# Gate block steps beside other units, ScalarE copies of the activations, weight sums ahead of the splits: a transformer block on one core

## The chip, the core and the metric

One core of a Trainium2 chip runs the whole layer in one launch. The metric is the device time in microseconds (us) of one execution. Times are medians of a few runs; one more execution is run under the profiler, and the trace is of that one.

## The reference, cut to what matters

```python
D_MODEL, SEQ, D_FF = 2048, 256, 5632          # all float32, batch 1, depth 1

def _swiglu(x, wg, wu, wd):
    return (jax.nn.silu(x @ wg) * (x @ wu)) @ wd

h = h + 0.5 * _swiglu(_rmsnorm(h, ffn1_norm), ffn1_wg, ffn1_wu, ffn1_wd)
...                                            # attention and short convolution, w_in, w_out
h = h + 0.5 * _swiglu(_rmsnorm(h, ffn2_norm), ffn2_wg, ffn2_wu, ffn2_wd)
g = jax.nn.sigmoid(_rmsnorm(h, ple_norm) @ ple_w_gate)
h = h + g * (p @ ple_w_proj)
out = _rmsnorm(h, final_norm)
```

The change touches the two SwiGLU stages only. Both are the same code, `swiglu`, called for ffn1 and for ffn2.

## The kernel before

**Tiling.** There are 256 tokens, so every product has two row tiles of 128 tokens (t = 0, 1). Activations are kept transposed, 16 blocks of 128 model columns in four chunks (`aTh[c]`, `aTl[c]`). Each float32 number is held as two parts, a rounded one (hi) and what is left (lo), and each product is three matmuls (`mm3`, lines 112 to 115): hi by hi, hi by lo, lo by hi. A weight tile is 128 x 1024: SyncE fetches it (`raw`), ScalarE copies it to `whi` (line 108), and VectorE subtracts to get `wlo` (line 109, called a split below). There are six buffers each for `raw`, `whi` and `wlo`.

**Units.** The 5632 hidden columns are 11 blocks of 512. A gate, up or down unit yields one 256 x 512 result, and consists of items: an item is one weight tile and 12 matmuls (`unit_items`). A gate or up unit has 8 items, a down unit 4 for each hidden block that it sums. Gate block 0 is computed plainly. Gate blocks 1 to 10 are computed as five pairs (`Pair`) by a Strassen-like scheme with seven products in place of eight. It needs sums of weight blocks and sums of activation blocks. A pair has 12 steps: steps 0 to 7 (short steps) fetch two weight tiles, VectorE makes three sums in them (lines 344 to 346), splits both, and TensorE runs 12 matmuls; steps 8 to 11 (long steps) fetch three tiles, make two sums (line 356), three splits and 18 matmuls. After step 7 `half` takes four of the products out of PSUM; after step 11 `whole` (lines 397 to 407) makes one ScalarE copy and six VectorE sums, and queues the silu of the four results.

**Activation sums.** `factors(nm, c, p)` (lines 295 to 319) takes one 128 x 512 piece of the activations, `a`, makes four VectorE differences of 128 x 128, a ScalarE copy (hi, `sh`) and a VectorE subtract (lo, `sl`). In ffn1, `a` comes from the loaded `xT` tile by two ScalarE copies (`ffn1sa`); in ffn2 from one VectorE addition of `aTh` and `aTl` (line 306). There are eight pieces a stage. The `xT` tiles share two buffers (tag "y").

**Order of the work.** `drive` (line 172) takes a stream of items and steps, written out by hand. It prepares ahead (fetch, sums, splits) until six weight tiles are held, and then runs the oldest. Each engine executes in the order in which this emits, so that everything on VectorE, ScalarE and SyncE is a queue. Smaller work (silu, transposes) waits in `queue`; one entry is taken after the matmuls of each item (`pump`). An up unit's result is multiplied into the gate by VectorE from PSUM (line 449), transposed by TensorE and split (`pair_major`), and is then an input of the down unit. Up and down units share two PSUM banks ("mm"), so a unit can start only when the one ahead of it has been taken out.

**The schedule before.** Stage opening: gate unit 0 (8 items), up unit 0, two empty items (at the second, the queue is emptied), four down units of block 0; the 12 steps of pair 0 lie between (`merge`, lists of counts at lines 516 and 521). Then, for i = 0 to 3, a period: the two up units of pair i, with a short step of pair i+1 after every two items, and then the four down units of pair i, with a long step of pair i+1 after every four. At the end the up and down units of pair 4 alone. In ffn1, `factors` for chunks 0 to 2 are called in the preparation of gate unit 0 (`early`, line 510) and chunk 3 in that of up unit 0 (line 486). In ffn2, gate unit 0's end calls `rstd_of` (a reduction of the sums of squares on VectorE, a power on GpSimd) and the silu of gate block 0 (`silu0`).

Of the kernel before, what the change touches and what calls it, by code (L numbers as in the profile page):

```python
# [3 lines left out]

# [19 lines left out]
SEQ = 256  # L24
# [9 lines left out]
def block_kernel(ctx, tc, x, xT, pT, cols, fin, bias, mask,  # L34
# [198 lines left out]
    def next_aT(which, c, p):  # L233
# [22 lines left out]
    xraw = {}  # L256

    def load_xT(c, k0, n):
# [5 lines left out]
        for k in range(k0, k0 + n):  # L264
# [3 lines left out]
                op0=ALU.mult, op1=ALU.subtract)  # L268

# [25 lines left out]
    def factors(nm, c, p, raw=None):  # L295
# [33 lines left out]
    class Pair:  # L329
# [7 lines left out]
        def prep(self, n):  # L337
# [11 lines left out]
            rs = [fetch(w[k0, 1], f"{nm}_0"), fetch(w[k0 + 1, 1], f"{nm}_1")]  # L349
# [47 lines left out]
        def whole(self):  # L397
# [15 lines left out]
            for t in range(2):  # L413
                queue.append(partial(silu, t))

    def swiglu(nm, nxt, wg, ws, wu, wd, first):
        gate = {}
        g0 = [wk(f"{nm}sg0_{t}") for t in range(2)]

        def merge(u, pr, sched):  # L420
            s_items = pr.items()
            for cnt in sched:
                for _ in range(cnt):
                    yield next(u)
                yield next(s_items)
            assert next(u, None) is None
# [11 lines left out]
        def silu0():  # L438
            gate["rstd"] = rstd_of(nm)
# [3 lines left out]
        def up(fc, g, dst, wide=False, late=None):  # L443
            def done(pu):
                if first and fc == 0:
                    silu0()
                gs = g()
                for t in range(2):
                    stt(out=gs[t], in0=pu[t], scalar=gate["rstd"][:, t:t + 1], in1=gs[t],
                        op0=ALU.mult, op1=ALU.mult)  # L450
                dst.append(big(fc - 1 & 1, f"{nm}g{fc}"))
                for p in range(2):
                    queue.append(partial(pair_major, gs, p, f"{nm}gT{fc}", dst[-1]))
            return unit_items(wu, fc, f"{nm}u{fc}", aT, done, wide=wide, late=late)
# [25 lines left out]
        def opening():  # L480
            sets = []
            if first:
                def late(g, s):
                    load_x(g) if s == 0 else None
                    if g == 0:
                        factors(nm, 3, s, xraw[3])
                yield from up(0, lambda: g0, sets, late=late)
            else:
                yield from gate0()
                yield from up(0, lambda: g0, sets)  # L490
# [4 lines left out]
        def period(i, pr, wide=False):  # L495
            sets = []
            for j in range(2):
                yield from up(1 + 2 * i + j, lambda j=j: [pr.c[j], pr.c[2 + j]], sets, wide)
            yield from down(1 + 2 * i, 2, sets, i == 4, wide)

        def early(g, s, nm_, src):
# [394 lines left out]
```

## Time and profile before

| | |
|---|---|
| median of 3 runs | 1990.82 us (1990.23 to 1991.31) |
| profiled execution | 1991.36 us, of which the trace spans 1988.9 us |
| TensorE busy, as modelled | 1921.4 us (97% of the span) |
| VectorE busy | 1486.4 us (75%) |
| ScalarE busy | 1042.1 us (52%) |
| mean granted TensorE clock | 0.989 of full speed |
| HBM read | 433 MB, 219 GB/s over the span |

A share of the span is a mean over stages. What a change in one stage is worth is read there: from the gaps of TensorE, what ended each, and what the queue of that engine held ahead of it.

### The profile page before, as it was taken

The numbers are of one execution on the slowest core, as the hardware profiler recorded it, in microseconds if no ns is written. First come the engines' busy times: TensorE is split into PE (matmuls) and PEld (weight loads), VectorE is DVE, ScalarE is ACT, GpSimd is POOL, SyncE is SP. The second block draws the span as 40 slices with busy tenths as digits, with TensorE's granted clock in tenths as the row PEclk, the third lists the DMA queues.
The fourth block names the chain that finished last, engine by engine and source line by source line (L and its number), as shares of the span: only waits on it lengthen the run. The fifth ranks groups of instructions, "written<-read, shape, count | busy, mean of one in ns | idle before, by whom it ended". The sixth has DMA issues, their size and how long they took to land. (4 is left out here: it accounts for less than half of the span.)

```text
span 1988.9 us, 23885 instructions
## 1 busy us (share of the span) xinstructions
PE 1921.4 (97%) x8649; PEld 1577.0 (79%) x8649; DVE 1486.4 (75%) x1720; ACT 1042.1 (52%) x1305; POOL 34.8 (2%) x36
## 2 busy tenths in 40 slices
PE   7899999999999999999999979999999999999998
PEld 4677788787887888888888868787878878788887
DVE  6889789788797655656556678987977978876664
ACT  5555545555455555555445545555545545554653
POOL 0000000000000000100000000000000000000010
PEclk8899999999999999999999989999999999999999
DMA  6677768677687755544555547777676866775652
GB/s 226 240 252 245 255 216 286 227 236 249 208 276 241 237 173 189 194 167 169 180 183 177 191 148 235 257 248 263 224 252 207 285 235 227 253 248 203 204 184 98
DMA packets 127206, 437.09 MB, mean 220 GB/s; under 512 B 13808, under 2 KB 14320, under 8 KB 126832
## 3 DMA queue, kind: packets, MB, share of 16 engines
q1 hardware_dynamic: 127088, 435.57, 64.3%
q8 instruction: 68, 1.11, 0.2%
q14 instruction: 50, 0.41, 0.1%
HBM read 433.41 MB, written 2.10 MB: 219 GB/s over the span
## 5 line engine op out<-in xcount | busy, mean ns | idle before, releaser
L44 ACT ACTIVATE whi_ffn2s<-raw_ffn2s 128x1024 fp32r<-128x1024 f32 x120 | 126.4, 1060 | 124.2 <-DVE raw_ffn2s L344 81.4
L44 ACT ACTIVATE whi_ffn1s<-raw_ffn1s 128x1024 fp32r<-128x1024 f32 x120 | 126.4, 1060 | 116.4 <-DVE raw_ffn1s L344 73.3
L109 DVE TENSOR_TENSOR wlo_ffn2s<-raw_ffn2s,whi_ffn2s 128x1024 fp32r<-128x1024 f32 x120 | 145.9, 1222 | 11.6 <-ACT whi_ffn2s L44 5.5
L109 DVE TENSOR_TENSOR wlo_ffn1s<-raw_ffn1s,whi_ffn1s 128x1024 fp32r<-128x1024 f32 x120 | 145.8, 1222 | 8.1 <-ACT whi_ffn1s L44 1.4
L113 PE MATMUL ffn2u<-whi_ffn2u,aTh 128*128 128x512 f32 x352 | 138.6, 394 | 12.0 <-ACT ffn2sg L44 11.9
L114 PE MATMUL ffn1u<-wlo_ffn1u,aTh 128*128 128x512 f32 x352 | 137.4, 390 | 2.9 <-DVE wlo_ffn1u L109 2.9
L113 PE MATMUL ffn1u<-whi_ffn1u,aTh 128*128 128x512 f32 x352 | 138.2, 393 | 0.6 <-ACT whi_ffn1u L44 0.5
L109 DVE TENSOR_TENSOR wlo_ffn2d<-raw_ffn2d,whi_ffn2d 128x1024 fp32r<-128x1024 f32 x88 | 106.6, 1223 | 42.0 <-ACT whi_ffn2d L44 40.5
L109 DVE TENSOR_TENSOR wlo_ffn1d<-raw_ffn1d,whi_ffn1d 128x1024 fp32r<-128x1024 f32 x88 | 106.6, 1223 | 41.8 <-ACT whi_ffn1d L44 40.1
L115 PE MATMUL ffn2u<-whi_ffn2u,aTl 128*128 128x512 f32 x352 | 137.7, 391 | 0.0
L114 PE MATMUL ffn2u<-wlo_ffn2u,aTh 128*128 128x512 f32 x352 | 137.7, 391 | 0.0
L115 PE MATMUL ffn1u<-whi_ffn1u,aTl 128*128 128x512 f32 x352 | 137.1, 390 | 0.0
L44 ACT ACTIVATE whi_ffn2d<-raw_ffn2d 128x1024 fp32r<-128x1024 f32 x88 | 92.0, 1057 | 70.2 <-PE ffn2d L115 33.7
L44 ACT ACTIVATE whi_ffn1d<-raw_ffn1d 128x1024 fp32r<-128x1024 f32 x88 | 92.3, 1057 | 68.7 <-PE ffn1d L115 33.6
L109 DVE TENSOR_TENSOR wlo_ffn2u<-raw_ffn2u,whi_ffn2u 128x1024 fp32r<-128x1024 f32 x88 | 104.5, 1219 | 21.1 <-ACT whi_ffn2u L44 20.7
L109 DVE TENSOR_TENSOR wlo_ffn1u<-raw_ffn1u,whi_ffn1u 128x1024 fp32r<-128x1024 f32 x88 | 104.6, 1219 | 20.1 <-ACT whi_ffn1u L44 20.1
L44 ACT ACTIVATE whi_ffn2u<-raw_ffn2u 128x1024 fp32r<-128x1024 f32 x88 | 89.2, 1049 | 23.6 <-PE ffn2d L115 11.2
L44 ACT ACTIVATE whi_ffn1u<-raw_ffn1u 128x1024 fp32r<-128x1024 f32 x88 | 89.2, 1048 | 21.4 <-PE ffn1d L115 11.2
L113 PEld LDWEIGHTS ffn2u<-whi_ffn2u,aTh 128*128 128x128 f32 x352 | 66.6, 189 | 26.4 <-ACT ffn2sg L44 12.3
L114 PEld LDWEIGHTS ffn1u<-wlo_ffn1u,aTh 128*128 128x128 f32 x352 | 66.3, 188 | 17.1 <-DVE wlo_ffn1u L109 3.5
L113 PEld LDWEIGHTS ffn1u<-whi_ffn1u,aTh 128*128 128x128 f32 x352 | 66.2, 188 | 15.3 <-ACT whi_ffn1u L44 1.3
L115 PEld LDWEIGHTS ffn2u<-whi_ffn2u,aTl 128*128 128x128 f32 x352 | 66.5, 189 | 14.0
(795 smaller groups left out, 5106.8 us busy)
## 6 DMA issues: line engine op xcount, KB each, us to landing
raw_ffn1s<-in_ws SPq DMA_DIRECT2D x120, 512.0 KB, 5.6
raw_ffn2s<-in_ws SPq DMA_DIRECT2D x120, 512.0 KB, 5.5
raw_ffn1u<-in_wu SPq DMA_DIRECT2D x88, 512.0 KB, 5.2
raw_ffn1d<-in_wd SPq DMA_DIRECT2D x88, 512.0 KB, 4.8
raw_ffn2u<-in_wu SPq DMA_DIRECT2D x88, 512.0 KB, 5.2
raw_ffn2d<-in_wd SPq DMA_DIRECT2D x88, 512.0 KB, 4.8
raw_o<-in_wout SPq DMA_DIRECT2D x32, 512.0 KB, 3.9
raw_pg<-in_wpg SPq DMA_DIRECT2D x24, 512.0 KB, 4.6
```

Source lines behind the costliest of these rows:

```text
L44: nc.scalar.activation(out=out, in_=in_, func=func, **kw)
L109: tt(out=lo[:, sl], in0=raw[:, sl], in1=f(hi[:, sl]), op=ALU.subtract)
L113: nc.tensor.matmul(ps, lhsT=xh, rhs=wh, start=first, stop=False)
L114: nc.tensor.matmul(ps, lhsT=xh, rhs=wl, start=False, stop=False)
L115: nc.tensor.matmul(ps, lhsT=xl, rhs=wh, start=False, stop=last)
```

## The change

The arithmetic of the products stays the same, with the same weights, matmuls and transposes. What is done otherwise:

1. The steps of a pair move. The short steps of pair i+1 now lie between the items of the down units of pair i (one after every two), and its long steps between the items of its own up units (before the 1st and 5th item of the first up unit, and the 1st and 3rd of the second). The places of the 60 steps of a stage are given as positions in one stream.
2. The first up unit of a pair (`up_a`) ends before the pair's gate. It is copied out of PSUM by ScalarE (`ua`); after the silu, `after` multiplies the two in SBUF on VectorE. The second (`up_b`) is multiplied from PSUM as before.
3. The two halves of a transposed hidden block are queued as one entry (`turned`) in place of two.
4. `factors` reads a ScalarE copy (`keep`, tiles `full`), made where the activations are made: in ffn1 right behind each `xT` load, in ffn2 from the PSUM tile of the transposes. All eight `factors` of ffn1 move to the preparation of up unit 0.
5. In ffn2, `rstd_of` is called before gate unit 0.
6. In the long steps the fetch of the third tile and the two sums come ahead of the splits of the other two.

```diff
@@ next_aT, line 246
+            if which == "ffn2":
+                keep(c, k, ps[:, kk * 256:(kk + 1) * 256], g)
@@ line 256
+    full = {}
+    def keep(c, k, src, g):
+        p = k // 2
+        if (c, p) not in full:
+            full[c, p] = wk(f"a{c}_{p}")
+        act(full[c, p][:, (k % 2) * SEQ:(k % 2 + 1) * SEQ], src, scale=g)
@@ load_xT, line 268
+            keep(c, k, raw[:, k, :], g)
@@ factors, line 295
-    def factors(nm, c, p, raw=None):
+    def factors(nm, c, p):
...
-        a = wk(f"{nm}sa{c}_{p}")
-        k = 2 * p
-        if raw is None:
-            tt(out=a, in0=f(aTh[c][:, k:k + 2, :].rearrange("p k s -> p (k s)")),
-               in1=f(aTl[c][:, k:k + 2, :].rearrange("p k s -> p (k s)")), op=ALU.add)
-        else:
-            for i in range(2):
-                act(a[:, i * SEQ:(i + 1) * SEQ], raw[:, k + i, :],
-                    scale=col[:, c * 4 + k + i:c * 4 + k + i + 1])
+        a = full.pop((c, p))
@@ Pair.prep, line 348
-            rs = [fetch(w[k0, 1], f"{nm}_0"), fetch(w[k0 + 1, 1], f"{nm}_1")]
             t1 = raw_tile(f"{nm}_t")
             nc.sync.dma_start(out=t1.rearrange("p (k c) -> p k c", k=2),
                               in_=w[k0:k0 + 2, 0, :, 0:512].rearrange("k p c -> p k c"))
-            us = [split(rs[d], f"{nm}_{d}") for d in range(2)]
+            rs = [fetch(w[k0, 1], f"{nm}_0"), fetch(w[k0 + 1, 1], f"{nm}_1")]
             for d in range(2):
                 sl = slice(d * 512, (d + 1) * 512)
                 tt(out=t1[:, sl], in0=t1[:, sl], in1=rs[d][:, 0:512], op=ALU.add)
+            us = [split(rs[d], f"{nm}_{d}") for d in range(2)]
@@ Pair.whole, line 413
             for t in range(2):
                 queue.append(partial(silu, t))
+            queue.append(self.after)
+            queue.append(self.turn)
@@ swiglu (merge, up, opening and period are taken out)
         def silu0():
-            gate["rstd"] = rstd_of(nm)
+            if first:
+                gate["rstd"] = rstd_of(nm)
...
+        def turned(gs, fc, dst):
+            dst.append(big(fc - 1 & 1, f"{nm}g{fc}"))
+            def turn(d=dst[-1]):
+                for p in range(2):
+                    pair_major(gs, p, f"{nm}gT{fc}", d)
+            return turn
+        def gated(pu, gs):
+            for t in range(2):
+                stt(out=gs[t], in0=pu[t], scalar=gate["rstd"][:, t:t + 1], in1=gs[t],
+                    op0=ALU.mult, op1=ALU.mult)
+        def up0(sets, late=None):
+            def done(pu):
+                if first:
+                    silu0()
+                gated(pu, g0)
+                queue.append(turned(g0, 0, sets))
+            return unit_items(wu, 0, f"{nm}u0", aT, done, late=late)
+        def up_a(fc, pr, sets):
+            def done(pu):
+                ua = [wk(f"{nm}ua{fc}_{t}") for t in range(2)]
+                for t in range(2):
+                    act(ua[t], pu[t], scale=gate["rstd"][:, t:t + 1])
+                pr.ua = ua
+            return unit_items(wu, fc, f"{nm}u{fc}", aT, done)
+        def up_b(fc, pr, sets):
+            def done(pu):
+                gs = [pr.c[1], pr.c[3]]
+                gated(pu, gs)
+                queue.append(turned(gs, fc, sets))
+            return unit_items(wu, fc, f"{nm}u{fc}", aT, done)
+        def pair(i):
...
+            def after():
+                for t in range(2):
+                    tt(out=pr.c[2 * t], in0=pr.ua[t], in1=pr.c[2 * t], op=ALU.mult)
+                pr.turn_a = turned([pr.c[0], pr.c[2]], 1 + 2 * i, pr.sets)
+        def opening(pr):
...
                 def late(g, s):
-                    load_x(g) if s == 0 else None
-                    if g == 0:
-                        factors(nm, 3, s, xraw[3])
+                    if s == 0:
+                        load_x(g)
+                    factors(nm, g, s)
...
+        def plain_stream(prs):
+            yield from opening(prs[0])
+            for i in range(5):
+                yield from down(1 + 2 * i, 2, prs[i].sets, i == 4, i == 4)
+                if i < 4:
+                    yield from ups(i + 1, prs[i + 1])
@@ early, line 509
-            if g > 0:
-                factors(nm, g - 1, s, xraw[g - 1])
@@ everything
             if first:
                 yield from gate0(early)
-                sched = [2, 2, 1, 1, 1, 1, 1, 1, 2, 2, 2, 2]
+                at = [6, 8, 9, 10, 12, 14, 16, 18, 20, 24, 26, 29]
+                base = 34
             else:
+                gate["rstd"] = rstd_of(nm)
...
-                sched = [4, 3, 2, 3, 2, 2, 1, 1, 2, 2, 2, 2]
+                at = [6, 8, 11, 14, 16, 17, 18, 20, 22, 24, 26, 34]
+                base = 42
...
+                places += [base + 32 * i + o for o in (0, 2, 4, 6, 8, 10, 12, 14, 16, 20, 24, 26)]
```

`opening` ends with the two up units of pair 0, and a step stands before the item of the stream that its place names. In ffn1 the stream begins behind gate unit 0, in ffn2 with it.

## Rows read from the trace of the kernel before

**Rows 1.** The page, part 1: busy us, share of the span, instructions.

```profile
PE 1921.4 (97%) x8649; PEld 1577.0 (79%) x8649; DVE 1486.4 (75%) x1720; ACT 1042.1 (52%) x1305; POOL 34.8 (2%) x36
```

**Rows 2.** TensorE's waits: waiter, releaser, total us, how many, longest.

```profile
PE ffn2u L113 <- ACT ffn2sg L44: 11.9, 1, 11.9
PE ffn1g L113 <- ACT whi_ffn1g L44: 10.3, 4, 3.5
PE ffn1s0q L113 <- ACT ffn1sg L44: 7.2, 1, 7.2
...
PE ffn1s1q L114 <- DVE wlo_ffn1s L109: 1.0, 1, 1.0
...
PE ffn1d L113 <- ACT ffn1g4h L44: 0.9, 1, 0.9
...
PE ffn1d L115 <- DVE ffn1g4l L203: 0.6, 1, 0.6
...
PE ffn1s3q L114 <- DVE wlo_ffn1s L109: 0.4, 1, 0.4
```

**Rows 3.** Stretches: length, busy us of PE, PEld, DVE, ACT, POOL; PEclk, DMA, GB/s.

```profile
6.80:46.20 39.40, 29.84 (x96) 21.61 (x96) 27.52 (x60) 23.28 (x48) 2.57 (x2) 0.83 0.64 223
...
63.30:69.40 6.10, 6.06 (x14) 4.84 (x15) 4.54 (x6) 3.76 (x5) 0.00 (x0) 0.50 0.88 342
...
409.00:538.80 129.80, 127.89 (x570) 104.95 (x569) 107.20 (x117) 67.88 (x71) 0.00 (x0) 1.00 0.72 243
```

**Rows 4.** Timeline of TensorE where two stretches end: start, us, instruction.

```profile
148.21 0.39 PE L113 MATMUL ffn1u<-whi_ffn1u,aTh 128*128 128x512 f32 x1
148.44 0.39 PE L114 MATMUL ffn1u<-wlo_ffn1u,aTh 128*128 128x512 f32 x1
...
408.98 0.39 PE L113 MATMUL ffn1u<-whi_ffn1u,aTh 128*128 128x512 f32 x1
```

**Rows 5.** Waits of SyncE's DMA queue, first 70 us.

```profile
SPq L262 <- ACT ffn1sa L44: 19.4, 2, 10.0
```

**Rows 6.** Timeline of ScalarE in up unit 0 of ffn1.

```profile
45.13 0.63 ACT L44 ACTIVATE ffn1sh<-ffn1sv 128x512 fp32r<-128x512 f32 x1 [1.21 <-DVE ffn1sv L317]
...
49.12 0.63 ACT L44 ACTIVATE ffn1sh<-ffn1sv 128x512 fp32r<-128x512 f32 x1 [1.61 <-DVE ffn1sv L317]
```

**Rows 7.** Timeline of VectorE, one short step and two up items.

```profile
327.00 0.68 DVE L344 TENSOR_TENSOR raw_ffn1s<-raw_ffn1s,raw_ffn1s 128x512 f32<-128x512 f32 x1
...
331.54 2.35 DVE L109 TENSOR_TENSOR wlo_ffn1u<-raw_ffn1u,whi_ffn1u 128x1024 fp32r<-128x1024 f32 x2
333.81 0.69 DVE L344 TENSOR_TENSOR raw_ffn1s<-raw_ffn1s,raw_ffn1s 128x512 f32<-128x512 f32 x1
```

**Rows 8.** Timeline of VectorE, the last sum of `whole`, pair 2 of ffn1.

```profile
411.23 0.69 DVE L407 TENSOR_TENSOR ffn1s2c<-ffn1s2q,ffn1s2c 128x512 f32<-128x512 f32 x1
```

**Rows 9.** Timeline of VectorE, gate block 0 of ffn1: `rstd_of`, gating, lo of its transposes.

```profile
97.76 0.21 DVE L224 TENSOR_REDUCE sm_ffn_None<-ss_ffn 128x1 f32<-128x4 f32 x2
...
101.15 0.68 DVE L344 TENSOR_TENSOR raw_ffn1s<-raw_ffn1s,raw_ffn1s 128x512 f32<-128x512 f32 x1
...
107.96 1.28 DVE L203 TENSOR_TENSOR ffn1g0l<-ffn1gT,ffn1g0h 128x512 fp32r<-128x512 f32 x2
```

**Rows 10.** Timeline of ScalarE at the start of the down units of pair 2.

```profile
484.45 1.06 ACT L44 ACTIVATE whi_ffn1s_t<-raw_ffn1s_t 128x1024 fp32r<-128x1024 f32 x1 [2.73 <-issue]
485.41 0.58 ACT L44 ACTIVATE ffn1g6h<-ffn1gT 128x512 fp32r<-128x512 f32 x1
```

**Rows 11.** Timeline of ScalarE, opening of ffn2.

```profile
1146.04 0.19 ACT L44 ACTIVATION_READ_ACCUMULATOR junk_ffn<-h 128x1 f32 x1
...
1149.26 0.47 ACT L44 ACTIVATE aTh<-trh_ffn,col 128x256 fp32r<-128x256 f32 x1 [0.55 <-DVE aTl L244]
...
1181.56 1.28 ACT L44 ACT_TABLE_LOAD   x1
1184.32 1.26 ACT L44 ACTIVATE ffn2sg<-ffn2g,rstd_ffn_None 128x512 f32<-128x512 f32 x2 [1.48 <-POOL rstd_ffn_None L230]
```

More of the change, by code (lines that the diff above doesn't have):

```diff
@@ L3 @@
 from functools import partial
+from itertools import chain
 import concourse.bass as bass
@@ L418, in swiglu @@
         g0 = [wk(f"{nm}sg0_{t}") for t in range(2)]
[L420 to L426, printed above, removed]
         def gate0(early=None, late=None):
@@ L444, in done @@
+        def gated(pu, gs):
[3 more added lines that the diff above has]
+        def up0(sets, late=None):
             def done(pu):
-                if first and fc == 0:
+                if first:
                     silu0()
-                gs = g()
-                for t in range(2):
-                    stt(out=gs[t], in0=pu[t], scalar=gate["rstd"][:, t:t + 1], in1=gs[t],
-                        op0=ALU.mult, op1=ALU.mult)
@@ L451, in done @@
[L451 to L454, printed above, removed]
+                gated(pu, g0)
[4 more added lines that the diff above has]
+                ua = [wk(f"{nm}ua{fc}_{t}") for t in range(2)]
+                for t in range(2):
+                    act(ua[t], pu[t], scale=gate["rstd"][:, t:t + 1])
+                pr.ua = ua
+            return unit_items(wu, fc, f"{nm}u{fc}", aT, done)
@@ new lines, in up_b @@
+        def up_b(fc, pr, sets):
[5 more added lines that the diff above has]
+        def pair(i):
+            pr = Pair(nm, ws, i, gate)
+            pr.sets = []
+            def after():
+                for t in range(2):
+                    tt(out=pr.c[2 * t], in0=pr.ua[t], in1=pr.c[2 * t], op=ALU.mult)
+                pr.turn_a = turned([pr.c[0], pr.c[2]], 1 + 2 * i, pr.sets)
+            pr.after = after
+            pr.turn = lambda: pr.turn_a()
+            return pr
@@ L456, in swiglu, with ups @@
+        def ups(i, pr):
+            yield from up_a(1 + 2 * i, pr, pr.sets)
+            yield from up_b(2 + 2 * i, pr, pr.sets)
         class Lazy:
@@ L478, in nothing @@
             return 0, None, lambda _: fn() if fn is not None else None
-        def opening():
+        def opening(pr):
             sets = []
@@ L483, in late @@
                 def late(g, s):
-                    load_x(g) if s == 0 else None
-                    if g == 0:
-                        factors(nm, 3, s, xraw[3])
-                yield from up(0, lambda: g0, sets, late=late)
+                    if s == 0:
+                        load_x(g)
+                    factors(nm, g, s)
+                yield from up0(sets, late)
             else:
                 yield from gate0()
-                yield from up(0, lambda: g0, sets)
+                yield from up0(sets)
             yield nothing()
@@ L493, in opening @@
             yield from down(0, 1, sets, False)
[L495 to L499, printed above, removed]
+            yield from ups(0, pr)
+        def plain_stream(prs):
[4 more added lines that the diff above has]
+                    yield from ups(i + 1, prs[i + 1])
         def early(g, s, nm_, src):
@@ L520, in everything @@
                         queue.append(partial(factors, nm, c, p))
-                sched = [4, 3, 2, 3, 2, 2, 1, 1, 2, 2, 2, 2]
-            pr = Pair(nm, ws, 0, gate)
-            yield from merge(opening(), pr, sched)
+                at = [6, 8, 11, 14, 16, 17, 18, 20, 22, 24, 26, 34]
+                base = 42
+            prs = [pair(i) for i in range(5)]
+            places = list(at)
             for i in range(4):
-                nx = Pair(nm, ws, i + 1, gate)
-                yield from merge(period(i, pr), nx, [2] * 8 + [4] * 4)
-                pr = nx
-            yield from period(4, pr, True)
+                places += [base + 32 * i + o for o in (0, 2, 4, 6, 8, 10, 12, 14, 16, 20, 24, 26)]
+            u = plain_stream(prs)
+            n = 0
+            steps = chain.from_iterable(pr.items() for pr in prs)
+            for place in places:
+                while n < place:
+                    yield next(u)
+                    n += 1
+                yield next(steps)
+            yield from u
         drive(everything())
```

1 line of the change is left out of this document (removed).

## Prediction, made before the changed kernel was run

> **What bounds the kernel now.** I read the busy times first: TensorE is busy 97% of the span, VectorE 75%, ScalarE 52% [rows 1]. Within a unit the matmuls start 0.227 us apart [rows 4], so an item or short step (12 matmuls) takes 2.72 us and a long step (18) 4.08; the change alters no matmul, so only TensorE's gaps can be won or added. They are 1988.9 - 1921.4 = 67.5 us in all. The table of TensorE's waits says where. First, single large gaps: gate unit 0 of ffn1 waits 10.3 us in four pieces for its copies, then 7.2 us for one ScalarE copy; up unit 0 of ffn2 waits 11.9 us for the silu of gate block 0 [rows 2]. Second, a small pattern: in each of the eight periods the first down unit waits 0.9 + 0.6 us for the second hidden block, and most periods begin with 0.4 to 1.2 us for a VectorE subtract [rows 2]. The table of stretches shows a whole period: 129.8 us with 127.9 of TensorE, so 1.9 to win [rows 3]. It shows, third, what a large gap costs besides itself: the granted clock was at 0.50 (the 1.2 GHz level) in the 6.1 us behind the 7.2 us gap, which is 3 us of work lost, and 0.83 on average in gate unit 0, whose longest gap is 3.5 us [rows 2, 3].
>
> So the sum has five terms. Each is how long VectorE and ScalarE, as queues, keep TensorE waiting in a stretch under the new order. My prices on VectorE: a pair of items and a short step 333.81 - 327.00 = 6.81, of which two items 2.27 (their row's 2.35 less the overlap at its end), so a short step 4.5 [rows 7]. TensorE needs 8.16 for the same.
>
> **1. Opening of ffn1.** Now the third and fourth chunk of `xT` wait 19.4 us in SyncE's queue until `ffn1sa` has read the first two [rows 5]. The copies by `keep` read them at once, so this wait goes, and six `factors` leave gate unit 0. An item of the gate unit then takes ScalarE two hi and two `keep` copies of 0.47 [rows 11] and two of half a tile, 1.06 / 2 [rows 10]: 2.9, or 2.65 with 0.05 of overlap at each, about TensorE's 2.72. At the 342 GB/s of the busiest row [rows 3] the inputs of five items, 0.79 MB each, and two bias tiles take 13 us, so I estimate the fifth item's landing at 17 and the gate unit's preparation to end at 28 (four items on); TensorE ends it at 31 in place of 46.
>
> But VectorE gets all eight `factors` in up unit 0. Such an item with its factor repeats every 49.12 - 45.13 = 4.0 us [rows 6], because subtract, differences, ScalarE copy and subtract wait for each other. From 28 on VectorE's queue is: first factor's copy at 31.4; seven more at 4.0, 28; squares and gate copies on ScalarE in between, 2; step 0, 4.5; to 66.9 with the last factor. Then steps 1 and 2, 9; `rstd_of` and gating, 101.15 - 97.76 = 3.4 [rows 9]; step 3, two down items, step 4, 4.5 + 2.3 + 4.5: 90.5. Only then comes the lo part of the transposed gate block (0.6 to its first half, 1.28 for both [rows 9]), because the preparation runs six tiles ahead and the transposes are emitted as the second empty item is run, behind step 4's preparation. The first down item needs it: TensorE, ready at 85, waits until 91, some 5.5 us, and I add 2.5 for the clock. The second down item ends at 91 + 2.3 + 2.7 + 2.5 = 98.5. Left are 26 units of 2.72, four long steps and transposes: 98.5 + 70.7 + 16.3 + 0.9 = 186.4. Now the same work is done at 148.2 [rows 4] plus 16 up items and transposes, 192.6. **Gain 6.3.** Bounds: -6 (half clock in the starved up unit as well, below) to +14 (the lo part is not late).
>
> **2. Periods, the gap that goes.** ScalarE copied the hi part of the second transposes (485.41) behind the copy of the third tile of a long step (484.45), which had waited for its sums [rows 10]. Behind the change both transposes are made after the first down item, a short step lies before they are needed, and weight sums come first. The wait at a period's start goes too: six up items now lie behind `whole`. Eight times 1.55, six times 0.35, two times 1.25 [rows 2]: **gain 17.0.**
>
> **3. Periods, the wait that is new.** `after` is taken from `queue` three items behind step 11, and VectorE has in front of it: `whole`, three up subtracts, and the next pair's step 0. `whole` ends 411.84 - 408.98 = 2.9 us behind step 11 [rows 4, 8]; three subtracts 3.4; step 0 4.5; two products of 0.6: 12.0. TensorE reaches the transposes of this block after four items, 10.9. So it stands 1.1 us, behind it everything else. The silus (ScalarE, done by 5) are not last. There is no step 0 behind pair 4, and in ffn2 pair 0 has eight items there; seven waits remain. **Loss 8.0.** No row shows this wait; the nearest ones are the 0.9 and the 1.4 + 1.1 us by which such queues are late now, so 0 to 2.5 each, 0 to 17 in all. In the down units VectorE needs 2 x 6.81 + 1.28 for two sums into `h` = 14.9 per four items and two steps, TensorE 16.3, so I cost it at nothing; it enters with six tiles in hand.
>
> **4. Opening of ffn2 to up unit 0.** `rstd_of` is now the first VectorE work of the stage, and the emission order chains everything of the stage behind it. It needs the squares of the last chunk, done at 1146.2 [rows 11], so subtracts that now are made ahead start at 1146.8, and TensorE stands 3 us there. `next_aT` of the last chunk gets `keep` copies. The second hi copy starts 0.55 us late, when VectorE's read of the same PSUM tile has ended [rows 11], so with `keep` the three reads of a column go one by one, 1.42 us in place of 1.03: 5.7 for four. VectorE's queue from 1146.8: six subtracts 6.8, four columns to 1158.3, step 0 4.5, two factors with items 8.0, two factors 5.1, step 1: its copy at 1177.7, its first subtract at 1179.2. TensorE gets there at 1173.2, waits, and ends step 1 at 1181.6. The silu is behind four copies and a table load (1.28), 1.26 long [rows 11]: done about 1184.4. Up unit 0 starts at 1184.1 in place of 1185.1, at full clock sooner: **gain 2.5**, -6 to +12 (nothing waits at 1145, and the silu finds its factor ready).
>
> The Trainium skill (PSUM — Partial Sum Buffer, "PSUM bank collisions raise a hardware error") says that no two engines may use one bank and quadrant at once, reads beside reads included. The rows agree: by it the sum is as above; if the copies could run beside VectorE, step 1 would be 1.6 us sooner and the total 1976.4.
>
> **5. Opening of ffn2, first down unit.** As in 1, the lo of gate block 0 is emitted behind the preparation of step 7. From the end of up unit 0: gating 0.8, step 6 4.5, two items 2.3, step 7 4.5, lo 0.6: 12.5; TensorE is there at 9.2. It waits 3.3, and I charge 2 for the clock, since the 3.5 us gap is the nearest. Now there are 0.9 us. **Loss 4.4**, 0 to 8.
>
> The rest I cost at nothing: `ua` (0.6 us copies) is hidden by the long step behind it, the gating of `up_b` by step 0, `h` by a short step each. DMA moves the same bytes. In the last down units the first one takes the other PSUM banks.
>
> **Sum** against the profiled execution: 1991.4 - 6.3 - 17.0 + 8.0 - 2.5 + 4.4 = **1978.0 us**. That execution lies 0.5 above the median, which is less than my rounding.
>
> **Rivals.** (a) The new waits don't come: ScalarE and VectorE reach `after` and the lo parts in time. For it: in term 3 the margin is 1 us, and TensorE has four items of cover. Against: three queues would have to be short at once. Without term 3, and with terms 1, 4 and 5 at +10, +4 and 0: 1960. (b) Openings give nothing: up unit 0 of ffn1 is starved to 68% for 35 us and its clock halves. Then an item takes 5.1 us in place of VectorE's 4.0, eight of them 9 us more: 1987. Against it: these gaps are of 1 to 2 us, half of the smallest behind which I saw it fall. The same time comes out if `xT` is not what paces gate unit 0, that is if the change doesn't do there what it says. (c) Slower: the products of `after` are later than I count, because VectorE comes late to step 11 by a preparation. Every 1 us more is 7 us in all. At 1.9 more, 3.0 each, the gain is gone; with two more items' subtracts in its way (2.3) it is 7 x 2.3, and at gaps of 3.4 us each 7 x 2 for the clock: 2008. For it speaks that VectorE runs without a pause for 60 us of a period now; against it, that these are short steps beside up items, and step 11 now has light work ahead.
>
> **How the numbers follow.** Forecast 0.53, (a) 0.16, (b) 0.19, (c) 0.12. The forecast's own range is 1969 to 1986, from its terms' bounds taken together. With 8 in 10 I reach from (a) to just above (b): 1961 to 1992. A difference under 0.2%, 4 us, can't be told from none: faster is the forecast, (a), and a little of (b), 0.71; same most of (b), 0.17; slower (c), 0.12.
>
> **What would show it.** The wait for `ffn1sa` gone from SyncE's queue, and gate unit 0 done by 31 to 33; TensorE waiting for `wlo` in up unit 0 with gaps of 1 to 2 us; one gap near 5 us at the first down item of ffn1, for `ffn1g0l`; none of 0.9 + 0.6 at the down units, and seven of about 1 us at transposes, released by VectorE's products; in ffn2 a gap of 3 us at 1145, one before step 1, one at the first down item, none of 11.9. I am wrong if the transposes wait 3 us or more, or if the clock is at half through up unit 0.

## The result, and the profile after

The changed kernel takes **1967.92 us** (median of 3, 1966.44 to 1968.21) against 1990.82: a ratio of 0.9883 (95% interval 0.9861 to 0.9906). The gain is 22.9 us; 13.4 were forecast. Its profiled execution took 1967.92 us with a span of 1965.8.

The page of the kernel after, part 1 (busy us, share of the span, instructions), answers to [rows 1]:

```profile
PE 1920.9 (98%) x8649; PEld 1583.5 (81%) x8649; DVE 1475.8 (75%) x1712; ACT 1054.9 (54%) x1341; POOL 36.2 (2%) x36
```

The same matmuls are busy for the same time; all that changed lies between them. TensorE's waits of the kernel after (waiter, releaser, total us, how many, longest), beside [rows 2]:

```profile
PE ffn2g L115 <- DVE wlo_ffn2g L110: 3.4, 1, 3.4
PE ffn1s0q L114 <- ACT whi_ffn1s L45: 3.2, 3, 2.0
PE ffn1s0q L115 <- DVE wlo_ffn1s L110: 3.1, 4, 1.0
PE ffn2d L114 <- ACT ffn2g0h L45: 2.4, 1, 2.4
PE ffn1g L114 <- ACT whi_ffn1g L45: 2.4, 1, 2.4
PE ffn1d L114 <- ACT ffn1g0h L45: 2.3, 1, 2.3
PE ffn2s0q L114 <- ACT whi_ffn2s L45: 2.3, 1, 2.3
PE ffn1u L115 <- DVE wlo_ffn1u L110: 2.2, 3, 0.8
...
PE ffn1gT L292 <- DVE ffn1s0c L483: 1.8, 2, 1.6
...
PE ffn1gT L292 <- DVE ffn1s1c L483: 0.8, 2, 0.6
```

Of the 11.9 before up unit 0 of ffn2 0.6 is left, and of the 10.3 in gate unit 0 one wait of 2.4 at its start; the 7.2 before step 0 and the sixteen waits of 0.9 and 0.6 are gone. In their place stand the waits that the prediction named: 3.4 at the start of ffn2, one before step 1 of ffn2 (`ffn2s0q`), one at each first down item, and one at the transposes of seven pairs (`ffn1s0c` 1.8, six others 0.8). The largest that it did not price is 6.3 in all at the first steps of pair 0 in ffn1 (`ffn1s0q`). A stretch of gate unit 0, the 24 us behind it with most of up unit 0, and one whole period, from one pair's first transpose to the next pair's, beside [rows 3]:

```profile
core 0: us, PE busy (x) PEld busy (x) DVE busy (x) ACT busy (x) POOL busy (x), PEclk, DMA share, GB/s
8.00:32.00 24.00, 24.00 (x95) 19.41 (x95) 19.05 (x36) 21.34 (x46) 0.00 (x0) 1.00 1.00 368
32.00:56.00 24.00, 19.71 (x75) 14.54 (x73) 17.30 (x31) 13.28 (x28) 3.16 (x2) 0.93 0.59 208
...
310.05:438.21 128.16, 127.34 (x569) 105.28 (x569) 106.41 (x117) 68.38 (x73) 0.00 (x0) 1.00 0.73 246
```

From 8 us on gate unit 0 of ffn1 now runs without a gap, with all DMA engines busy. The period is 128.16 us in place of 129.8. (A down unit has two items for each hidden block that it sums, so four in a period, and not four for each block.)

**Where the time came from.** The last matmul of the output projection ends 13.5 us sooner (1130.25 against 1143.72), and from there to the first matmul behind ffn2 (`pp`) it is 9.6 us less (726.2 against 735.8). So ffn1 gives 13.5 and ffn2 9.6, where the terms of the forecast make 10.2 and 3.2.

### The profile page after: what moved, and what is told of

It reads as the page before. It is cut to its first block, busy times and chain, and to the rows that moved or that the text cites. A ratio compares the mean times of both kernels' runs of the same rounds, so it can differ in the third digit from the quotient of the medians.

```text
span 1965.8 us, 23881 instructions
## 1 busy us (share of the span) xinstructions
PE 1920.9 (98%) x8649; PEld 1583.5 (81%) x8649; DVE 1475.8 (75%) x1712; ACT 1054.9 (54%) x1341; POOL 36.2 (2%) x36
## 4 chain that ended last, share of the span: by engine, by line
PE 88%; DVE 6%; ACT 3%; issue 2%; DMA 1%; ACTq 0%; POOL 0%; SPq 0%; POOLq 0%; DVEq 0%
PE ffn1d L116 4%; PE ffn2d L116 4%; PE ffn2d L114 4%; PE ffn1d L114 4%; PE ffn2d L115 4%; PE ffn1d L115 4%; PE ffn2u L114 4%; PE ffn2u L116 4%; PE ffn2u L115 3%; PE ffn1u L114 3%; PE ffn1u L116 3%; PE ffn1u L115 3%; PE o L116 1%; PE o L114 1%; PE o L115 1%
## 5 line engine op out<-in xcount | busy, mean ns | idle before, releaser
L110 DVE TENSOR_TENSOR wlo_ffn1d<-raw_ffn1d,whi_ffn1d 128x1024 fp32r<-128x1024 f32 x88 | 104.6, 1220 | 11.1 <-ACT whi_ffn1d L45 10.3
L114 PEld LDWEIGHTS ffn2u<-whi_ffn2u,aTh 128*128 128x128 f32 x352 | 66.1, 188 | 14.8 <-ACT ffn2sg L45 1.3
L116 PEld LDWEIGHTS ffn1u<-whi_ffn1u,aTl 128*128 128x128 f32 x352 | 66.7, 189 | 13.9
```

The costliest lines, as they stand in the source:

```text
L110: tt(out=lo[:, sl], in0=raw[:, sl], in1=f(hi[:, sl]), op=ALU.subtract)
L114: nc.tensor.matmul(ps, lhsT=xh, rhs=wh, start=first, stop=False)
L116: nc.tensor.matmul(ps, lhsT=xl, rhs=wh, start=False, stop=last)
```

## Experiments

Each time is a median of four runs with the kernel before on the same chip; ratios are to that. The runs were made on four chips, and the kernel before had medians of 1989.99 to 1991.53 us there, so a difference between two kernels from different chips is good to 1 or 2 us. All spans and stretches come from one trace each.

### Which part brings it: the sums or the schedule

My theory for the periods named both: ScalarE's copy of the third tile waits for the sums, and the moved steps take the transposes out of its way. Two kernels separate them. The kernel before with the sums first alone:

```diff
-            rs = [fetch(w[k0, 1], ...), fetch(w[k0 + 1, 1], ...)]
             t1 = raw_tile(f"{nm}_t")
             nc.sync.dma_start(out=t1..., in_=w[k0:k0 + 2, 0, :, 0:512]...)
-            us = [split(rs[d], f"{nm}_{d}") for d in range(2)]
+            rs = [fetch(w[k0, 1], ...), fetch(w[k0 + 1, 1], ...)]
             for d in range(2):
                 tt(out=t1[:, sl], in0=t1[:, sl], in1=rs[d][:, 0:512], op=ALU.add)
+            us = [split(rs[d], f"{nm}_{d}") for d in range(2)]
```

> The kernel before with one part of the change alone: in the four long steps of a pair the two weight sums stand ahead of the first two splits. Theory A (the 0.9 + 0.6 us at the first down unit of a period come from ScalarE's copy of the third tile, which waits for sums that stand behind two subtracts): these sixteen waits go, 12.4 us as listed and up to 4 more if each wait also costs a refill of some 0.27 us that the table of waits does not count; 1974 to 1980. Theory B (the waits come from where the long steps and the second transposes lie in the order, and only the moved steps take them away): within 2 us of the kernel before, 1989 to 1991, waits of 0.9 + 0.6 still there.

Measured: **1971.32 us** (0.9905, 0.989 to 0.992). And the changed kernel with these lines as they were before (the same diff backwards):

> The changed kernel with the weight sums of the long steps behind the two splits again, as before: the schedule of the change without the sums. The kernel before with the sums alone gave 1971.3, a steady period of 128.2 us instead of 129.8. Theory A (sums first is what the periods live on; the moved steps bring nothing by themselves): 1978 to 1984, periods of 129 us or more. Theory B (either of the two takes the 0.9 + 0.6 us away, since the moved steps take the transposes out of the way of the third tile's copy): 1967 to 1971, periods near 128.2.

Measured: **1977.85 us** (0.9931, 0.9915 to 0.9948). So the sums alone gain 18.7, the schedule and the rest alone 13.7, both together 22.9: they overlap, and the few lines of the sums are the larger part. VectorE's subtract of the third tile shows why; the last part is the idle time ahead of its twenty instructions in ffn1. The kernels before, with the schedule alone, with the sums alone, and after:

```profile
L109 DVE TENSOR_TENSOR wlo_ffn1s_t<-raw_ffn1s_t,whi_ffn1s_t 128x1024 fp32r<-128x1024 f32 x20 | 24.5, 1225 | 25.1 <-ACT whi_ffn1s_t L44 25.1
```

```profile
L110 DVE TENSOR_TENSOR wlo_ffn1s_t<-raw_ffn1s_t,whi_ffn1s_t 128x1024 fp32r<-128x1024 f32 x20 | 24.5, 1225 | 25.1 <-ACT whi_ffn1s_t L45 25.1
```

```profile
L109 DVE TENSOR_TENSOR wlo_ffn1s_t<-raw_ffn1s_t,whi_ffn1s_t 128x1024 fp32r<-128x1024 f32 x20 | 24.5, 1223 | 9.4 <-ACT whi_ffn1s_t L44 9.4
```

```profile
L110 DVE TENSOR_TENSOR wlo_ffn1s_t<-raw_ffn1s_t,whi_ffn1s_t 128x1024 fp32r<-128x1024 f32 x20 | 24.4, 1221 | 3.2 <-ACT whi_ffn1s_t L45 3.1
```

With the sums behind two subtracts VectorE stands still for 25.1 / 20 = 1.26 us in each long step, since subtract, sums, copy and subtract follow each other. The moved schedule leaves this bubble as it is: the first matmul of an up item then waits for a bank that VectorE empties late, 0.9 us a period (`h` as releaser), where the kernel before waited 0.9 and 0.6 for transposes. With sums first alone two small waits a period are left. TensorE's waits in the middle of ffn1, schedule alone, then sums alone:

```profile
PE ffn1u L114 <- DVE h L509: 3.8, 4, 1.2
```

```profile
PE ffn1s2q L114 <- DVE wlo_ffn1s L109: 0.4, 1, 0.4
...
PE ffn1d L115 <- DVE ffn1g2l L203: 0.2, 1, 0.2
```

Theory A held for the sums in its mechanism, and the gain was larger than its range by 2.7 us; that rest isn't assigned. Of the second run theory A held in its time (0.15 below its range) and its period (129.24), but its words that the moved steps bring nothing by themselves did not: here too the waits of 0.9 and 0.6 are gone, only others of 0.9 and 0.8 stand in their place, and the kernel gains 13.7. And one thing that neither expected: a period with sums alone is 128.20 us, with the whole change 128.16. **In steady state the moved steps, as they stand in the change, bring nothing over the sums**, and in ffn2 as a whole they and the rest don't either (725.6 against 726.2 us); what they give back in waits at down items they spend at the new transposes. What the schedule, the copies and the moved `factors` have of their own is the 4.2 us in ffn1, whose opening they shorten.

### The new wait at the transposes, and what a wait costs

Theory: the two products of `after` stand behind the next step 0's sums and subtracts. First, that step one item later:

```diff
-at = [6, 8, 9, 10, 12, 14, 16, 18, 20, 24, 26, 29]
+at = [6, 8, 9, 10, 12, 14, 16, 18, 20, 24, 26, 28]
-places += [base + 32 * i + o for o in (0, 2, 4, ...)]
+places += [base + 32 * i + o for o in (1, 2, 4, ...)]
```

> The changed kernel with the first step of the next pair one item later (and step 11 of pair 0 in ffn1 one item sooner), so that the two products stand ahead of that step's sums on VectorE. Theory A (the products are late by what VectorE has to prepare ahead of them): all seven waits at the transposes go. The table lists 6.7 us for them; if a wait costs 0.16 us ahead of it and 0.2 to 0.3 behind it on top of what is listed, the gain is 9.5. So 1958.5 against 1961.2 tells whether the listed time is the whole cost. Theory B (it is the silu or the ua copy, or the step moved is late in its turn): 1965 to 1968, the waits still there or as much at the first step of a pair.

Measured: **1961.88 us** (0.9860, 0.9845 to 0.9874), 6.0 less than the changed kernel. The seven waits are gone (theory A), but a small one of 0.26 stands at eight first down items, since the transposes end too close ahead of them. So the run doesn't decide between 1958.5 and 1961.2: with these eight taken off, listed waits alone would give 4.6 us, and 5.7 with the prices that the table below gives, too near to each other for two chips. The periods in that table decide it.

One of the eight:

```profile
PE ffn1d L114 <- DVE ffn1s1c L451: 0.3, 1, 0.3
```

So the same effect by another edit, which also brings the transposes one item forward (like the run above and all kernels built on this one, it has step 11 of pair 0 in ffn1 one item sooner, 28 in place of 29):

```diff
-            for t in range(2):
-                queue.append(partial(silu, t))
+            queue.append(lambda: (silu(0), silu(1)))
             queue.append(self.after)
```

> The changed kernel with both silus of a pair as one entry of the queue (and step 11 of pair 0 in ffn1 one item sooner): products and transposes both come one item earlier. In the run with step 0 one item later the waits at the transposes went, but 0.26 us at the first down item came in their place, for the hi half of this block. Theory A (that hi half was one item short of time): no wait at the transposes nor at the first down item, 1958 to 1960. Theory B (VectorE reaches the products too late for transposes that are one item earlier): 1962 to 1968, waits for products at the transposes.

Measured: **1960.33 us** (0.9844, 0.983 to 0.9859), 7.6 less, theory A, 0.3 above its range; between 100 and 680 us TensorE has no wait at all, and elsewhere three of 0.21 at transposes are left. Its period of 126.91 us is 1.29 below that of the sums alone: with this edit the moved steps do bring something in steady state. It is the yardstick for the others. Period from the first transpose of pair 1 to that of pair 2 in ffn1 (the two gaps of 0.60 and 0.21 at one pair's transposes count as one wait of 0.81):

| kernel | waits listed in it, us | how many | period, us | over 126.91 |
|---|---|---|---|---|
| before | 0.91 + 0.64 + 0.35 = 1.90 | 3 | 129.80 | 2.89 |
| schedule alone | 0.81 + 0.88 = 1.69 | 2 | 129.24 | 2.33 |
| sums alone | 0.22 + 0.36 = 0.58 | 2 | 128.20 | 1.29 |
| after | 0.81 | 1 | 128.16 | 1.25 |
| step 0 later | 0.26 | 1 | 127.43 | 0.52 |
| silus together | none | 0 | 126.91 | 0 |

Every period is longer than its listed waits by 0.26 to 0.44 us for each of them. The records around a wait show it, here TensorE at a transpose wait of the kernel after (start us, length, line, operation, tiles, count, idle before and releaser):

```profile
308.84 0.39 PE L115 MATMUL ffn1u<-wlo_ffn1u,aTh 128*128 128x512 f32 x1
309.06 0.39 PE L116 MATMUL ffn1u<-whi_ffn1u,aTl 128*128 128x512 f32 x1
310.05 0.30 PE L292 MATMUL ffn1gT<-ident,ffn1s1c 128*128 128x128 f32 x1 [0.60 <-DVE ffn1s1c L483]
310.56 0.98 PE L292 MATMUL ffn1gT<-ident,ffn1s1c 128*128 128x128 f32 x7 [0.21 <-DVE ffn1s1c L483]
```

Back to back, matmuls start 0.22 to 0.23 apart. Here 0.99 lie between the last one and the transpose: 0.60 are listed as idle, and 0.16 more are the end of a matmul that otherwise lies beside the next one's start. The transposes behind the wait start further apart as well. **A wait that TensorE runs into costs its listed time and about 0.27 us** (0.44 for the two gaps at one pair's transposes).

### The opening of ffn1: the factors or the release of `xT`

Term 1 said that gate unit 0 was held by `xT`'s slow release and by six `factors`. First the changed kernel with these six back in gate unit 0, `xT` still free at once:

```diff
             out = split(raw, nm_, 2)
+            if g > 0:
+                factors(nm, g - 1, s)
...
-                    factors(nm, g, s)
+                    if g == 0:
+                        factors(nm, 3, s)
```

> The changed kernel with the factors of the first three chunks of xT back in gate unit 0 of ffn1, where the kernel before had them, but still from the copies, so that xT is free at once. Theory A (the opening is bound by VectorE's sum of work, wherever the factors lie): gate unit 0 ends at 36 to 40 us instead of 32.5, up unit 0 has no waits, and the whole is 1964 to 1969. Theory B (xT's release alone paced gate unit 0 and its factors cost nothing there): it still ends by 33, the waits of up unit 0 and of step 0 go: 1957 to 1961. Theory C (factors in gate unit 0 make it the bound): 1971 or more.

Measured: **1970.25 us** (0.9894, 0.988 to 0.9909). Gate unit 0 ends at 45.6, 13 us later, and yet the whole is only 2.3 longer: theory C in the gate unit, and in the whole between the ranges of A and C. Then the other cause, as it was meant: the kernel before with sums first and the differences of the `factors` on GpSimd, `xT` released as slowly as it was:

```diff
+    pt = nc.gpsimd.tensor_tensor
-        tt(out=v[:, 0], in0=a21, in1=a22, op=ALU.subtract)
+        pt(out=v[:, 0], in0=a21, in1=a22, op=ALU.subtract)
```

(and so for the other three)

> The kernel before with the weight sums first (1971.3 us) and the differences of the factors on GpSimd; none of the moved steps, copies or reductions of the change. Theory A (VectorE's work in the factors is what paced gate unit 0 of ffn1, whatever the schedule): gate unit 0 ends at 34 to 38 us in place of 46, the 5.6 us before step 0 shrink: 1956 to 1963. Theory B (in the old schedule xT's slow release paces the gate unit, so the factors' cost is hidden): gate unit 0 still ends near 46, 1968 to 1972.

Measured: **1978.21 us** (0.9942, 0.9925 to 0.9958), slower than the sums alone by 6.9. Gate unit 0 still ends at 46.8, as theory B said, but the time is 6 us above its range: up unit 0 of ffn2 waits 15.2 us in place of 11.9, and ffn1 is 2.9 longer than with the sums alone. The last starts of gate unit 0, and what stood in the way: SyncE's queue, and VectorE's subtract of the factors (idle time ahead of it, 8 to 66 us). After; factors back; before; sums and GpSimd:

```profile
L114 PE MATMUL ffn1g<-whi_ffn1g,aTh x32: 388/390/794, 7.6 to 31.6; 128*128 128x512 f32 x32
```

```profile
L114 PE MATMUL ffn1g<-whi_ffn1g,aTh x32: 387/396/628, 7.5 to 44.1; 128*128 128x512 f32 x32
...
SPq L100 <- DVE wlo_ffn1g L110: 15.4, 4, 4.3
```

```profile
L319 DVE TENSOR_TENSOR ffn1sl<-ffn1sv,ffn1sh 128x512 fp32r<-128x512 f32 x8 | 5.8, 729 | 7.4 <-ACT ffn1sh L44 4.9 <-ACT ffn1sa L44 2.5
```

```profile
L114 PE MATMUL ffn1g<-whi_ffn1g,aTh x32: 389/397/795, 7.2 to 45.9; 128*128 128x512 f32 x32
...
PE ffn2u L114 <- ACT ffn2sg L44: 15.2, 1, 15.2
...
SPq L263 <- ACT ffn1sa L44: 20.0, 2, 10.4
...
L320 DVE TENSOR_TENSOR ffn1sl<-ffn1sv,ffn1sh 128x512 fp32r<-128x512 f32 x8 | 6.2, 780 | 20.9 <-ACT ffn1sh L44 16.6 <-ACT ffn1sa L44 4.3
```

With the factors back, the wait for `ffn1sa` of [rows 5] is gone from SyncE's queue; it waits for VectorE's subtracts instead, and TensorE ends the unit as late as before. So the six factors alone are enough for the 46 us. What they cost is their chain: copy, differences, copy (`ffn1sh`) and subtract go from engine to engine, and the hi copies of successive weight tiles start 5.17 us apart, where TensorE needs 2.72 for a tile. Freeing `xT` does give something that TensorE doesn't show: the last hi copy of the unit starts at 38.9 in place of 42.5, but the granted clock is at 0.50 from 39.8 to 46.6.

The run with GpSimd does not isolate the other cause. It takes the differences off VectorE but leaves them in the chain, and VectorE stands idle 20.9 us ahead of the factors' subtract in place of 7.4. The hi copies of successive tiles start 5.34 us apart where no transfer is waited for, against 4.5 in the kernel before. **That the factors in gate unit 0 hold it is shown; that the slow release of `xT` would hold it alone is not.** First down items show what counts further on: 90.4 us in the kernel after and 92.3 with the factors back, though gate unit 0 ends 13 us later. That agrees with VectorE's work bounding this opening wherever it lies, so less of it should show at once under the new schedule.

### Less work for VectorE, and the start of ffn2

In ffn2 the reductions of `rstd_of` stood ahead of six subtracts that could have been made earlier:

```diff
-                gate["rstd"] = rstd_of(nm)
...
-                yield from gate0()
+                def stat(g, s):
+                    if (g, s) == (2, 1):
+                        gate["rstd"] = rstd_of(nm)
+                yield from gate0(late=stat)
```

> The changed kernel with the reductions of ffn2's scale emitted behind the first six preparations of gate unit 0 instead of ahead of all. Theory A (the 3.4 us at the start of ffn2 and the half clock behind it are the price of a VectorE queue that stands behind the last squares): the wait goes, VectorE is 6 us sooner through the gate unit, 1961 to 1964. Theory B (VectorE's work up to the silu is what counts, and the time comes back in front of step 1 or of the silu): 1966 to 1968, with a longer wait there.

Measured: **1961.60 us** (0.9854, 0.9838 to 0.9871), 6.3 less: theory A. The 3.4 us are gone, and the wait before step 1 is what it was, not longer (2.3). With the silus together as well:

> The changed kernel with the silus as one entry and with the reductions of ffn2's scale behind the first six preparations. The two touch different stretches, so theory A: gains add, 6.3 of the reductions and 6 to 9.5 of the silus: 1952 to 1956. Theory B (one of them only moves a wait): 1958 to 1962.

Measured: **1955.44 us** (0.9820, 0.9805 to 0.9834), 12.5 less than the change: the two nearly add. On this kernel, the four differences on GpSimd:

> The kernel with silus together and reductions later (1955.4 us), with the four differences of every factor (128x128, 0.28 us each on VectorE) made on GpSimd, in both openings. Theory A (the openings are bound by VectorE's sum of work): 1.1 us less for each of eight factors in ffn1 and four in ffn2, waits of up unit 0 and of the first steps smaller, first down item of ffn1 4 to 8 us earlier: 1946 to 1951. Theory B (VectorE's queue stands still while it waits for the differences, so what GpSimd takes longer comes back): 1954 to 1962, VectorE idle before the factors' subtract.

Measured: **1935.88 us** (0.9725, 0.971 to 0.9739), a further 19.6, more than twice what I expected. Theory A's mechanism, mis-sized: I had taken 1.1 us for a factor. In this kernel `a` is made early, and GpSimd runs ahead of VectorE: the differences of five factors are done by 21.8 us, while gate unit 0 is still running. VectorE's groups up to 90 us, without and then with GpSimd:

```profile
L322 DVE TENSOR_TENSOR ffn1sl<-ffn1sv,ffn1sh 128x512 fp32r<-128x512 f32 x8 | 5.5, 693 | 6.4 <-ACT ffn1sh L45 6.4
...
L317 DVE TENSOR_TENSOR ffn1sv<-a 128x128 f32<-128x128 f32 x8 | 3.4, 421 | 0.0
L318 DVE TENSOR_TENSOR ffn1sv<-a 128x128 f32<-128x128 f32 x8 | 3.4, 421 | 0.0
...
L319 DVE TENSOR_TENSOR ffn1sv<-a,ffn1sv 128x128 f32<-128x128 f32 x8 | 2.3, 292 | 0.3
L320 DVE TENSOR_TENSOR ffn1sv<-a,ffn1sv 128x128 f32<-128x128 f32 x8 | 2.3, 292 | 0.3
```

```profile
L323 DVE TENSOR_TENSOR ffn1sl<-ffn1sv,ffn1sh 128x512 fp32r<-128x512 f32 x8 | 6.0, 752 | 3.0 <-ACT ffn1sh L45 3.0
```

The differences are 3.4 + 3.4 + 2.3 + 2.3 = 11.4 us, and VectorE stood 6.4 us waiting for its own chain to come back from ScalarE; now 3.0. That is 14.8 us of its queue, and the output projection ends 13.0 sooner. ffn2 gives 6.8: the wait before step 1 and the half clock behind it are gone.

### The first down item

Both openings have a wait of some 3 us at the first down item. Theory: the lo half is emitted behind a step. First the changed kernel with one step moved:

```diff
-at = [6, 8, 9, 10, 12, 14, 16, 18, 20, 24, 26, 29]
+at = [6, 8, 9, 10, 14, 16, 17, 18, 20, 24, 26, 29]
-at = [6, 8, 11, 14, 16, 17, 18, 20, 22, 24, 26, 34]
+at = [6, 8, 11, 14, 16, 17, 18, 22, 23, 24, 26, 34]
```

> The changed kernel with one gate block step in each opening moved behind two more down items (ffn1: step 4 from place 12 to 14, ffn2: step 7 from 20 to 22, the next ones closed up), so that the lo half of the first transposed gate block stands behind two subtracts of 1.15 us instead of a whole step of 4.5. Theory A (order of emission makes the first down item wait): both waits fall from 3.0 to about 0.8 us and the half clock behind them goes, 4.4 + 2 to 3.4 us: 1960 to 1962. Theory B (VectorE has a backlog there, so the step that was moved is late instead): 1965 to 1968, with new waits at that step.

Measured: **1966.85 us** (0.9882, 0.9867 to 0.9896), 1.1 less, which is within the scatter: theory B. The waits split up and move on. TensorE at the first down items of ffn1, kernel after, then this one:

```profile
PE ffn1d L114 <- ACT ffn1g0h L45: 2.3, 1, 2.3
PE ffn1d L116 <- DVE ffn1g0l L204: 0.6, 1, 0.6
```

```profile
PE ffn1d L114 <- DVE h L509: 2.4, 2, 1.6
PE ffn1d L116 <- DVE ffn1g0l L204: 1.4, 1, 1.4
```

Then ffn2's steps spread over more items (`[6, 8, 11, 13, 16, 17, 20, 22, 23, 24, 26, 34]`, on the kernel of 1955.44):

> The same kernel (1955.4 us) with the gate block steps of ffn2's opening spread: step 3 one item sooner, step 6 behind the second down item, step 7 behind the fourth. VectorE then has one step and two items in front of the lo half of the first gate block, 6.8 us, in place of 11.3. Theory A (five steps close together are more than VectorE can do beside them): the 2.7 + 0.65 us at the first down item and the half clock behind go, 1950.5 to 1952.5. Theory B (as where the step alone was moved back: the lateness moves to the next items): 1954 to 1956.

Measured: **1953.26 us** (0.9813, 0.9797 to 0.983): 2.2 less, between the theories (the intervals of the two ratios overlap; in the traces ffn2 takes 715.9 us in place of 718.5); 1.8 + 1.0 us are left of 2.7 + 0.65. At last all of these together, ffn1's steps sooner too (`[4, 6, 8, 9, 10, 13, 16, 18, 20, 24, 26, 28]`):

> The kernel with silus together, reductions later and the differences on GpSimd (1935.9 us), with the steps of both openings spread: ffn2's as in the run before (it gave 2.2 us), ffn1's from 6, 8, 9, 10, 12, 14 to 4, 6, 8, 9, 10, 13, since VectorE is now free in up unit 0. Theory A (VectorE's lateness at the first down item is the last large gap, 4.6 us with half clock behind it in ffn1): that gap falls below 2, ffn2's as in the run before: 1927 to 1931. Theory B (transfers or VectorE in up unit 0 are the next bound): waits come back in up unit 0, 1933 to 1936.

Measured: **1935.36 us** (0.9727, 0.9713 to 0.9742), no different from the 1935.88: theory B. The 4.6 us at the first down item become 0.6, and 2.9 at a step ahead of it and 2.7 at a later down item take their place. Order alone did little in these three runs, where VectorE has a backlog; what helped was less work on it.

## Why the prediction was right, and where it was off

The direction and the places of all five terms came out, and the time lies in the range of 1961 to 1992 that was given 8 in 10; the sum was 9.5 us short, 1.1 below the forecast's own range. Its sums have small slips: seven of 1.1 are 7.7, where term 3 has 8.0, and by the prices given the columns of term 4 end at 1159.3, where 1158.3 is written. By its terms, with the two errors that the runs priced:

| term | forecast, us | measured, us |
|---|---|---|
| 1 opening of ffn1 | +6.3 | +5.8 |
| 2 waits gone in the periods | +17.0 | 17.0 listed, + 26 x 0.27 = 24.0 |
| 3 transposes | -8.0 | 6.7 listed, + 7 x 0.44 = -9.8 |
| 4 and 5, opening of ffn2 | -1.9 | -1.5 |
| half clock in a period of before | not counted | +1.6 |
| sum | +13.4 | +20.1, of 23.1 in the spans |

**The step that failed** is the price of a gap in terms 2 and 3: I took the listed wait for the whole cost. Twenty-six waits went and seven came; with what stands around them the two terms came out 5.2 us better. Another 1.6 us lay in one period of the kernel before, 131.43 us long in place of 129.8, whose granted clock was at 0.50 (the 1.2 GHz level) for 3.4 us behind two of the waits; I had taken all eight periods for alike. Some 3.0 us stay open. About 1.4 of them lie in the periods: these prices make one 2.71 - 1.25 = 1.46 us shorter, and the traces show 129.80 - 128.16 = 1.64, eight times.

```profile
1475.73:1479.14 3.41, 3.41 (x10) 2.67 (x9) 2.51 (x4) 0.60 (x1) 0.00 (x0) 0.50 0.82 286
1432.26:1563.69 131.43, 129.53 (x570) 106.11 (x568) 107.39 (x118) 67.86 (x72) 0.00 (x0) 0.99 0.72 240
```

**Term 1.** Forecast for gate unit 0 was an end at 31 and for the second down item 98.5; it is 32.5 and 98.5. The way there was another: the first down item waited 3.0 and not 5.5, but the granted clock was at half in four stretches between 50.9 and 95.2, 20 us in all, also behind gaps of 0.7 to 1.3 us in up unit 0. Rival (b) named this, and I had argued against it that these gaps were too small to make the clock fall. That argument was wrong, and the trace of before already spoke against it: the lines above show the clock at half behind waits of 0.9 and 0.6. It cost little here by luck: TensorE reached the first down item at 88.1 in place of 85, but VectorE's lo part began at 91.1 (90.5 forecast), so that TensorE only waited less. Of the two causes that I gave for gate unit 0 the factors are shown; what the slow release of `xT` is worth alone stays open.

**Term 2.** The mechanism was right, the attribution loose. I gave three reasons for the gap to go (transposes later, a step in between, sums first) and one is enough for all but 0.58 of the 1.90 us listed in a period: the sums.

**Term 3.** Right in kind, place and number: six of 0.81 and one of 1.85, released by VectorE's products, against 1.1. Rival (c), the lateness that grows, didn't come: the six are equal to 0.01 us.

**Terms 4 and 5.** 3.4 us at the start (3 forecast), up unit 0 starts 40.6 us behind the projection's end (40.5), the first down item waits 3.0 (3.3). The three reads of a PSUM column go one by one, as the rows had it: ScalarE's first copies of two columns start 1.40 apart (1.42 forecast). This agrees with the Trainium skill (PSUM — Partial Sum Buffer, "PSUM bank collisions raise a hardware error"), by which two engines must not use one bank and quadrant at once, reads included. ScalarE, then VectorE, kernel after:

```profile
1140.08 0.47 ACT L45 ACTIVATE aTh<-trh_ffn,col 128x256 fp32r<-128x256 f32 x1 [7.32 <-PE trh_ffn L239]
1141.11 0.47 ACT L45 ACTIVATE a<-trh_ffn,col 128x256 f32<-128x256 f32 x1 [0.55 <-DVE aTl L245]
1141.48 0.47 ACT L45 ACTIVATE aTh<-trh_ffn,col 128x256 fp32r<-128x256 f32 x1
...
1140.59 0.48 DVE L245 SCALAR_TENSOR_TENSOR aTl<-trh_ffn,col,aTh 128x256 fp32r<-128x256 f32 x1 [0.63 <-ACT aTh L45]
```

## What to carry to other kernels

Look first for an engine that stands still inside one instruction chain (idle time ahead of a group, released by an engine that waits for it in turn): here moving two sums ahead of two splits gave four fifths of what a whole new schedule with them gave. Price a gap at its listed wait and what stands around it. Where an engine has a backlog, moving its work mostly moves the wait; take work off it, to an engine that is idle. But see first that the idle engine can run ahead: the same four differences on GpSimd gave 19.6 us where their input was ready early, and the kernel became 6.9 us slower where VectorE's queue stood idle until they were made.

## What the runs showed of the hardware

**VectorE and GpSimd slow each other.** With the differences on GpSimd, VectorE's subtracts of half a tile beside them take 0.94 us at the median in place of 0.69, and GpSimd's 128x128 operations between 0.46 and 1.44. Of the sixteen subtracts of gate unit 0 the ten that lie beside a GpSimd instruction take 0.76 to 0.95, the six others 0.68 to 0.69. Up to 32 us, kernel after, then with GpSimd (min/median/max ns), and GpSimd's instructions in up unit 0:

```profile
L110 DVE TENSOR_TENSOR wlo_ffn1g<-raw_ffn1g,whi_ffn1g x16: 683/691/693, 7.5 to 27.2; 128x512 fp32r<-128x512 f32 x16
```

```profile
L111 DVE TENSOR_TENSOR wlo_ffn1g<-raw_ffn1g,whi_ffn1g x16: 675/941/953, 7.4 to 27.1; 128x512 fp32r<-128x512 f32 x16
...
38.23 1.44 POOL L319 TENSOR_TENSOR ffn1sv<-a 128x128 f32<-128x128 f32 x1
39.74 0.46 POOL L320 TENSOR_TENSOR ffn1sv<-a,ffn1sv 128x128 f32<-128x128 f32 x1
```

The Trainium skill (SBUF — State Buffer, "SBUF: two separate sides") says that a VectorE operation with two SBUF inputs and a GpSimd operation that reads SBUF lock one pair of ports against each other for a whole instruction. The rows agree in that both grow; it was worth it all the same here, for GpSimd is nearly idle in these openings (2% of the span) and VectorE had a backlog.

**The clock can fall behind small gaps too**: the granted clock was 0.50 in two stretches, 50.9 to 54.3 and 57.7 to 64.5 us of the kernel after, behind waits of 0.7 to 2.0 us, and in one period of the kernel before behind 0.9 and 0.6, while seven periods with the same waits kept 1.00. What decides between the two isn't shown. Kernel after, in the columns of [rows 3]:

```profile
40.00:50.00 10.00, 7.27 (x28) 4.72 (x26) 6.32 (x14) 7.09 (x15) 0.00 (x0) 1.00 0.52 167
50.00:60.00 10.00, 6.29 (x16) 4.54 (x16) 9.13 (x12) 3.69 (x4) 3.16 (x2) 0.71 0.21 60
60.00:70.00 10.00, 9.84 (x34) 7.51 (x32) 8.15 (x16) 3.69 (x5) 0.00 (x0) 0.77 0.59 202
```
